# Both opening projections of a layer with the tokens stationary, and one transpose of the gated convolution input in place of two

## The chip, the cores and the metric

The kernel runs on one core of a Trainium2 chip. The metric is the device time of one execution in microseconds (us): 2051.56 us before the change, the median of three runs from 2049.41 to 2052.84.

The core's engines work side by side, each through its own queue in order: TensorE multiplies matrices into PSUM (PE in the profile; its loads of the stationary operand are PEld), VectorE (DVE) and ScalarE (ACT) do elementwise work, GpSimd (POOL) and SyncE (SP) here issue most DMAs.

## The reference, cut to what matters

A trunk of two layers on 256 tokens of width 2048. Each layer normalises its input, multiplies it by one wide weight matrix, and runs three branches on slices of the product: a sparse attention (A), a convolution (B) and a stick-breaking attention (C). Each branch is gated and projected, the three are merged by sigmoid gates, and an output projection is added to the input.

```python
h = rms_norm(x, norm_w)
proj = h @ w_in
(qa, ka, va, za, qi, ki, wi, ub, zb, qc, kc, vc, zc, gates) = jnp.split(proj, split_points(), axis=-1)

def conformer_conv(u, conv_w, conv_b, ln_w, ln_b):
    a, gt = jnp.split(u, 2, axis=-1)
    y = a * jax.nn.sigmoid(gt)
    y = depthwise_causal_conv(y, conv_w, width=31) + conv_b   # 1024 channels, along the tokens
    y = layer_norm(y, ln_w, ln_b)
    return jax.nn.silu(y)

y_b = (conformer_conv(ub, ...) * jax.nn.silu(zb)) @ w_b_out
```

What the change touches is `a * sigmoid(gt)`: 1024 channels of `a` and 1024 of `gt`, both slices of `proj`, multiplied and handed to a convolution that runs along the tokens. Everything is float32.

## The kernel before

**Precision.** Each factor of a large product is split into a high part, rounded to the matmul format, and the remainder, the low part. A product is the sum of three matmuls: high by high, low by high, high by low. ScalarE makes the high part of a weight (`high`, L219, tile `wh`), VectorE subtracts it (`low`, L223, tile `wl`).

**Units.** Weights stream through SBUF in units, mostly of two blocks of 128 rows by 512 columns (0.5 MB). SyncE loads a unit into `raw` (four buffers), `high` and `low` convert it (three buffers each), TensorE uses it. `count[0]` counts loaded units, and delays in the code are given in units.

**Two orientations.** `chunk_N` makes a product of 512 output features for 256 tokens with the activations as the stationary operand: per unit 12 matmuls, each streaming 512 columns of the weight. The result has tokens on the partitions. `chunk_T` and `chunk_first` keep the weight stationary and stream the tokens, and their result has features on the partitions. All matmuls are issued by `mult` (L233).

**The opening of a layer.** Two chunks of 512 features are computed before the normalised input exists: the first half of the gate `gt` (`ga`), then the first half of `a` (`ua`). `chunk_first` multiplies the input that is scaled by the norm's weight alone (`ux`), in 24 matmuls of 256 columns per unit, while the sum of squares is still on its way. The missing factor, one number per token, is computed meanwhile: `rsqrt_mean`, then a diagonal matrix of it (`diag_cols`, L358, tile `dg`), and one matmul with a matrix of ones (`spread`, L499) that lays it along all partitions (`rb`). In layer 0 the sum of squares is collected by VectorE (L577, L628, L629) and summed by four small matmuls (L591) in the last unit of the first chunk. In layer 1 the last quarter of the input comes from the layer before and is transposed by TensorE (L436) after the first unit. During the second chunk, `follow` makes the normalised input `hx` unit by unit (`scale_x` L484 and L487, the high copy L489, `low_x` L494), and also finishes the gate: at unit 3 VectorE multiplies `ga` by `rb` (L513) and ScalarE takes the sigmoid (L514), at unit 5 VectorE multiplies by `rb` again (L518). Behind the second chunk VectorE multiplies `ua` by that gate (L684) straight into `yT`, the convolution's input with channels on partitions. In the opening VectorE's order is the written one (in the first chunk of layer 0 also ScalarE's and TensorE's); everything else is ordered by a planner from priorities, with weight conversion at high priority.

**The second half of the convolution's input.** It comes from two `chunk_N` products with tokens on partitions, so each is turned. `turned` lets VectorE transpose blocks of 32x32 (L264, tile `zt`), stores them by four POOL DMAs to DRAM (L267, `z`), and two units later loads them back with features on partitions (L272, `zy`). A given number of units after the product (`LATER` = 9, or more or less) the data is used. `use_g` takes the sigmoid of the turned gate on ScalarE (L402), `use_a` multiplies the turned `a` by it on VectorE into `yT` (L677).

**Taps.** The convolution is 31 multiply-adds per channel block on VectorE (L420, L422). `taps` appends them, one or two to an entry, to the list `waiting`; each conversion of a unit (`low`, through `drain`) emits one entry, except during the indexer's projections. What is left is emitted at once by `flush`. Then `conv_norm` (L910 to L935) normalises in stages between units. In branch order A, C, B, both come in the second group of 512 of branch C (`j == 1`).

**Other uses of a turn that matter here.** The rotary embedding of the queries (`rope_F`) begins with two ScalarE copies of turned data (L370, L371); `use_q` scales turned data (L788); a branch's gate takes a sigmoid (L402), two VectorE products (L409, L410) and a split (L362, L363).

Of the kernel before, what the change touches and what calls it, by code (L numbers as in the profile page):

```python
# [25 lines left out]
TAPS = 31  # L26
PRE = 2
LATER = 9
EV, EV2 = (3,), (5,)
URGENT = 10 ** 6  # L30
PAD = TAPS - 1
EPS = 1e-6
# [17 lines left out]
def trunk(ctx: ExitStack, tc: tile.TileContext, x, w_in, xt, w_a, w_b, w_c, w_out,  # L50
# [29 lines left out]
    def heads(a, n):  # L80
        return a.unsqueeze(1).to_broadcast([a.shape[0], n, a.shape[-1]])
# [24 lines left out]
    def part(b, i, k, n=1, ts=slice(0, S)):  # L106
        return b[k // 4][:, k % 4:k % 4 + n, i, ts]
# [124 lines left out]
    def mult(o, lhsT, rhs, start, stop):  # L232
        newest[0] = nc.tensor.matmul(o, lhsT, rhs, start=start, stop=stop, skip_group_check=True)  # L233
        return newest[0]
# [44 lines left out]
    def by_feature(y):  # L279
        return y.rearrange("p u k i -> p k u i")  # L280

    def blocks(v):
        return v.rearrange("p k (u i) -> p k u i", i=32)

    def chunk_F(w, c0, act, nk, use, later=LATER):
        turned(chunk_N(w, [(c0, 512)], act, nk), use, later)
# [14 lines left out]
    def chunk_first(act, units):  # L301
        acc = acc_tile()
        for k0 in range(0, KD, 2):
            ks, between = units(k0)
            order = [(n, u) for n in range(3) for u in ks]
            if between:
                order = [(n, u) for u in ks for n in range(2)] + [(2, u) for u in ks]
            for m, (n, (k, w_)) in enumerate(order):
                if m == len(ks) and between:
                    between()  # L310
                j, i = ((0, 0), (0, 1), (1, 0))[n]
                for f in range(4):
                    mm = mult(acc[:, f // 2, (f % 2) * S:(f % 2) * S + S], w_[j][:, f * P:(f + 1) * P],
                              part(act, i, k)[:, 0, :], k == 0 and n == 0 and f % 2 == 0,
                              k == KD - 1 and n == 2)
            background(mm)
        return [acc[:, i, :].rearrange("p (h t) -> p h t", h=2) for i in range(2)]

    def token_products(accs, n, w_, act, k0, ku, nk, ts):
        for i, j in ((0, 0), (1, 0), (0, 1)):  # L320
# [7 lines left out]
    def chunk_N(w, segs, act, nk, ku=2):  # L328
        acc = acc_tile()
        n = sum(c for _, c in segs)  # L330
        accs = [acc[:, t, :] for t in range(NT)]
        for k0 in range(0, nk, ku):
            background(token_products(accs, n, unit(w, k0, ku, segs), act, k0, ku, nk, range(NT)))
        return accs

    def rsqrt_mean(ssum, n, buf=None):
        w_ = ssum.shape[-1]
        if buf is None:
            buf = small(8)[:, :4 * w_]
# [14 lines left out]
    def diag_cols(r):  # L354
        dg = tp.tile([P, S], F32, tag="dg", bufs=1, name=nm("dg"))
        with tc.high_priority(offset=URGENT):
            for t in range(NT):
                nc.vector.tensor_scalar(dg[:, t * P:(t + 1) * P], ident, r[:, t:t + 1], None, op0=ALU.mult)  # L358
        return dg
# [40 lines left out]
    def sigmoid_of(y):  # L400
        sg = t4().rearrange("p (u k i) -> p u k i", k=4, i=32)
        nc.scalar.activation(sg, y, AF.Sigmoid)  # L402
        return sg
# [48 lines left out]
    def ssq_total(ssq):  # L452
        s = small(2)[:, :ssq.shape[1]]
        with tc.high_priority(offset=URGENT):
            nc.vector.reduce_sum(s, ssq, axis=AX.X)
        return s
# [13 lines left out]
    for layer in range(DEPTH):  # L470
# [8 lines left out]
        with tc.manual_schedule(engines={nc.vector.engine}), ExitStack() as order:  # L479
# [24 lines left out]
            def follow(k0):  # L504
                u = k0 // 2
                if u:
                    scale_x(u - 1)
                if u > 1:
                    low_x(u - 2)
                if u in EV:  # L510
                    for i in range(2):
                        s3 = sgs[i].rearrange("p (h t) -> p h t", h=2)
                        nc.vector.tensor_mul(s3, ga[i], heads(rb, 2))  # L513
                        nc.scalar.activation(sgs[i], sgs[i], AF.Sigmoid)  # L514
                if u in EV2:
                    for i in range(2):
                        s3 = sgs[i].rearrange("p (h t) -> p h t", h=2)
                        nc.vector.tensor_mul(s3, s3, heads(rb, 2))  # L518
                return advance_units(k0)[0], None if u else lambda: spread(state["dg"])

            todo = [(k, 2, seg[0]) for k in range(0, KD, 2)] + [(k, 2, seg[1]) for k in range(0, KD, 2)]
# [66 lines left out]
            def total_square():  # L588
                ps = mm_tile()
                for t in range(NT):  # L590
                    nc.tensor.matmul(ps[:, t:t + 1], state["sum"][:, t * P:(t + 1) * P], ones[:, :1], start=True, stop=True)  # L591
                state["dg"] = diag_cols(rsqrt_mean(ps[:, :NT], D))

            def start_0(k0):
                if k0 == 0:
# [36 lines left out]
            def start_1(k0):  # L632
                if k0 == 2:
                    x_parts(x_turn(tail), xn, 12, nw, 4)
                if k0 == 14:
                    state["dg"] = diag_cols(rsqrt_mean(ssq_total(ssq), D))
                return advance_units(k0)

            if layer == 0:
# [21 lines left out]
        def taps(j, yT=yT, cv=cv, pr=pr):  # L661
            ops = []
            for c in range(j * 4, j * 4 + 4, 2):
                for q in range(TAPS):
                    for d in range(2):
                        ops.append(partial(tap, yT, cv, pr, c + d, q))
            while ops:
                n = 1 + (len(waiting) % 2 == 0)
                waiting.append([4, ops[:n]])
                ops = ops[n:]  # L670

        def use_g(y):
            sg_u.append(sigmoid_of(y))
            yield 0

        def use_a(y, yT=yT):
            nc.vector.tensor_mul(blocks(yT[:, 4:8, PAD:]), by_feature(y), by_feature(sg_u.pop()))  # L677
            taps(1)
            yield 0

        sg_u = []
        with tc.high_priority():
            for i in range(2):
                nc.vector.tensor_mul(yT[:, i * 2:i * 2 + 2, PAD:], ua[i], sgs[i].rearrange("p (h t) -> p h t", h=2))  # L684
        taps(0)
        chunk_F(w, O_UG + 4 * P, hx, KD, use_g)
        chunk_F(w, O_UA + 4 * P, hx, KD, use_a, LATER + 2)


        qi = [slot(F32R).rearrange("p a b -> p (a b)").rearrange("p (h t) -> p h t", t=P) for _ in range(2)]  # L690
# [264 lines left out]
        for b in (0, 2, 1):  # L955
            if b == 2:
                finish()
                settle()
                gc = parts(KC)
                gate(O_ZC, qcT, gc, w, hx)  # L960
            if b == 1:
                finish()
                settle()
                gb = parts(KC)
                gate(O_ZB, cv, gb, w, hx)
                mx = parts(KD)
            gx = ga if b == 0 else gc if b == 2 else gb
            for j in range(4):
                if b == 2 and j == 1:
                    finish()  # L970
                    flush()
                    start(conv_norm())
                g = chunk_N(w, [(O_G + b * D + j * 512, 512)], hx, KD)
                sg = [ev() for _ in range(NT)]
                with tc.high_priority():
                    for t in range(NT):
                        nc.scalar.activation(sg[t], g[t], AF.Sigmoid)  # L977
                if j == 0:
                    settle()
                y = chunk_N((w_a, w_b, w_c)[b][layer], [(j * 512, 512)], gx, KC)  # L980
                with tc.high_priority():
                    for t in range(NT):
                        dst = mg[j // 2][:, j % 2, t, :]
                        if b == 0:
                            nc.vector.tensor_mul(dst, y[t], sg[t])
                        else:
                            nc.vector.tensor_mul(sg[t], y[t], sg[t])  # L987
                            nc.vector.tensor_add(dst, dst, sg[t])  # L988
                if b == 1 and j < 3:
                    turned([mg[j // 2][:, j % 2, t, :] for t in range(NT)], partial(use_m, j))  # L990
                elif b == 1:
                    start(turn(j))
# [140 lines left out]
```

## Time and profile before

| | |
|---|---|
| median of three runs | 2051.56 us (2049.41 to 2052.84) |
| the profiled execution | 2050.71 us, of which the span from first to last instruction is 2048.9 |
| TensorE matmuls | 2036.2 us busy (99%), 10080 |
| TensorE weight loads | 1738.4 us (85%) |
| VectorE | 1496.9 us (73%), 2022 instructions |
| ScalarE | 1036.1 us (51%), 1217 |
| POOL | 113.1 us (6%), 189 |
| granted TensorE clock | 0.999 |
| DMA traffic | 433.00 MB, 211 GB/s on average |

Rows of a timeline give the start in us from the span's start, the duration in us (for several merged instructions, of all), the engine, the line, the operation, the tiles written and read, the shape and the count. In brackets stands how long the engine was idle before it and what ended that. A matmul's recorded duration includes its way through the pipeline; how fast matmuls follow one another is read from the starts. Layer 0 runs from 0 to about 1022 us, layer 1 from there to the end; the openings lie at 5 to 54 us and at 1022 to 1070 us.

### The profile page before, as it was taken

The numbers are of one execution on the slowest core, as the hardware profiler recorded it, in microseconds if no ns is written. First come the engines' busy times: TensorE is split into PE (matmuls) and PEld (weight loads), VectorE is DVE, ScalarE is ACT, GpSimd is POOL, SyncE is SP. The second block draws the span as 40 slices with busy tenths as digits, with TensorE's granted clock in tenths as the row PEclk, the third lists the DMA queues.
The fourth block names the chain that finished last, engine by engine and source line by source line (L and its number), as shares of the span: only waits on it lengthen the run. The fifth ranks groups of instructions, "written<-read, shape, count | busy, mean of one in ns | idle before, by whom it ended". The sixth has DMA issues, their size and how long they took to land.

```text
span 2048.9 us, 26913 instructions
## 1 busy us (share of the span) xinstructions
PE 2036.2 (99%) x10080; PEld 1738.4 (85%) x10080; DVE 1496.9 (73%) x2022; ACT 1036.1 (51%) x1217; POOL 113.1 (6%) x189
## 2 busy tenths in 40 slices
PE   9999999999999999999999999999999999999998
PEld 9899888888888888888898998888888888888887
DVE  8778998688777855655676899886887677556555
ACT  7465445466444544444454654454664445444443
POOL 0100011010000001010101001110100000011000
PEclk9999999999999999999999999999999999999999
DMA  7777577675567667876767776776755766677864
GB/s 257 228 237 216 165 240 212 196 224 165 177 197 223 195 195 225 265 234 218 243 202 230 232 199 172 247 208 195 222 165 179 207 218 192 195 237 245 252 198 147
DMA packets 245860, 433.00 MB, mean 211 GB/s; under 512 B 19552, under 2 KB 69728, under 8 KB 245600
## 3 DMA queue, kind: packets, MB, share of 16 engines
q1 hardware_dynamic: 231632, 389.32, 62.7%
q0 software_dynamic: 12432, 38.81, 6.3%
q10 hardware_dynamic: 1664, 3.15, 0.4%
q8 instruction: 79, 1.29, 0.2%
q14 instruction: 53, 0.43, 0.1%
HBM read 407.62 MB, written 23.59 MB: 210 GB/s over the span
## 4 chain that ended last, share of the span: by engine, by line
PE 47%; DVE 2%; issue 1%; DMA 0%; ACT 0%; DVEq 0%; POOLq 0%
PE acc L233 46%; DVE wl L223 1%; DVE s L422 0%; DVE sc L773 0%; PE mm L800 0%; DMA zy<-z 0%; DVE sc L726 0%; PE mm L825 0%; PE mm L894 0%; PE mm L858 0%; DVE sm L725 0%; ACT wh L219 0%; PE mm L817 0%; PE mm L880 0%; PE mm L861 0%
## 5 line engine op out<-in xcount | busy, mean ns | idle before, releaser
L233 PE MATMUL acc<-wh,s 128*128 128x512 f32 (+2 forms) x4992 | 1220.0, 387 | 1.9 <-ACT wh L219 1.9
L223 DVE TENSOR_TENSOR wl<-raw,wh 128x1024 fp32r<-128x1024 f32 (+2 forms) x729 | 876.7, 1207 | 411.8 <-ACT wh L219 409.9
L219 ACT CAST wh<-raw 128x1024 fp32r<-128x1024 f32 (+2 forms) x728 | 756.8, 1043 | 802.0 <-PE acc L233 524.2
L233 PEld LDWEIGHTS acc<-wh,s 128*128 128x128 f32 x4992 | 922.5, 188 | 187.7 <-ACT wh L219 3.0
L233 PE MATMUL acc<-wl,s 128*128 128x512 f32 (+2 forms) x2496 | 658.7, 386 | 0.6 <-DVE wl L223 0.6
L233 PEld LDWEIGHTS acc<-wl,s 128*128 128x128 f32 x2496 | 462.9, 188 | 97.6 <-DVE wl L223 4.3
L422 DVE SCALAR_TENSOR_TENSOR s<-yT,cst,s 128x256 f32<-128x256 f32 x480 | 216.2, 477 | 0.4
L233 PE MATMUL acc<-s,wh 128*128 128x256 f32 (+2 forms) x1120 | 193.4, 319 | 0.9 <-ACT wh L219 0.9
L267 POOL DMA_DIRECT2D z<-zt x148 | 86.3, 590 | 1629.0 <-DVE zt L264 1482.8
L233 PEld LDWEIGHTS acc<-s,wh 128*128 128x128 f32 x1120 | 168.4, 190 | 4.5 <-ACT wh L219 1.1
L233 PE MATMUL acc<-s,wl 128*128 128x192 f32 (+1 forms) x864 | 115.3, 276 | 0.0
L233 PEld LDWEIGHTS acc<-s,wl 128*128 128x128 f32 x864 | 112.1, 191 | 0.9
L264 DVE STREAM_TRANSPOSE zt<-acc 128x512 f32<-128x512 f32 x56 | 39.8, 710 | 14.9 <-PE acc L233 14.6
L272 POOL DMA_DIRECT2D zy<-z x37 | 26.6, 719 | 191.2 <-DMA z<-zt 121.6
L362 ACT CAST s<-zy 128x1024 fp32r<-128x1024 f32 x18 | 18.9, 1050 | 34.2 <-DMA zy<-z 17.2
L987 DVE TENSOR_TENSOR ev<-acc,ev 128x512 f32<-128x512 f32 x32 | 22.0, 687 | 17.2 <-PE acc L233 17.2
L363 DVE TENSOR_TENSOR s<-zy,s 128x1024 fp32r<-128x1024 f32 x18 | 22.0, 1223 | 16.1 <-ACT s L362 16.1
L402 ACT ACTIVATE t<-zy 128x1024 f32<-128x1024 f32 x14 | 14.9, 1061 | 29.6 <-DMA zy<-z 29.6
L409 DVE TENSOR_TENSOR zy<-zy,t 128x1024 f32<-128x1024 f32 x12 | 14.7, 1221 | 16.2 <-ACT t L402 16.2
L977 ACT ACTIVATE ev<-acc 128x512 f32<-128x512 f32 x48 | 26.3, 590 | 0.0
L387 DVE TENSOR_TENSOR ev<-ev,cst 128x384 f32<-128x384 f32 (+2 forms) x20 | 11.2, 558 | 20.4 <-ACT ev L385 20.3
L988 DVE TENSOR_TENSOR s<-s,ev 128x512 f32<-128x512 f32 x32 | 21.9, 683 | 0.0
(207 smaller groups left out, 818.1 us busy)
## 6 DMA issues: line engine op xcount, KB each, us to landing
raw<-in_w_in_dram SPq DMA_DIRECT2D x555, 512.0 KB, 3.8
raw<-in_w_out_dram SPq DMA_DIRECT2D x64, 512.0 KB, 4.7
z<-zt POOLq DMA_DIRECT2D x148, 128.0 KB, 4.4
zy<-z POOLq DMA_DIRECT2D x37, 512.0 KB, 4.9
raw<-in_w_a_dram SPq DMA_DIRECT2D x32, 512.0 KB, 3.8
raw<-in_w_c_dram SPq DMA_DIRECT2D x32, 512.0 KB, 4.4
raw<-in_w_b_dram SPq DMA_DIRECT2D x32, 512.0 KB, 5.2
raw<-in_w_in_dram SPq DMA_DIRECT2D x16, 256.0 KB, 2.9
```

The lines of the kernel that those rows point to most:

```text
L219: newest_parts[0] = nc.scalar.copy(u[1], u[0])
L223: newest_parts[1] = sub = nc.vector.tensor_sub(u[2], u[0], u[1].bitcast(F32))
L233: newest[0] = nc.tensor.matmul(o, lhsT, rhs, start=start, stop=stop, skip_group_check=True)
L264: nc.vector.transpose(tmp[:, t].rearrange("p b k i -> p k b i"), src.rearrange("p (k b c) -> p k b c", b=4, c=32))
L267: nc.gpsimd.dma_start(z[:, :, :, a, :].rearrange("t b c e -> c (t b) e"), tmp[a * 32:(a + 1) * 32].rearrange("c t b k i -> c (t b) (k i)"))
L272: nc.gpsimd.dma_start(y.rearrange("p (t a) k i -> p t (a k i)", t=n), z.rearrange("t b c a e -> (b c) t (a e)"))
L362: nc.scalar.copy(h, src)
L363: nc.vector.tensor_sub(l, src, h.bitcast(F32))
L422: nc.vector.scalar_tensor_tensor(o, yT[:, c, q:q + S], wq, o, op0=ALU.mult, op1=ALU.add)
L977: nc.scalar.activation(sg[t], g[t], AF.Sigmoid)
L987: nc.vector.tensor_mul(sg[t], y[t], sg[t])
L988: nc.vector.tensor_add(dst, dst, sg[t])
```

## The change

`chunk_first` now keeps the tokens stationary, as `chunk_N` does: per unit 12 matmuls of 512 columns in place of 24 of 256. Its two results have tokens on the partitions, where the missing factor of the norm is one number per partition (`state["r"]`). So ScalarE's sigmoid of `ga` takes it as its scale, and VectorE multiplies `ua` by the factor and the gate in one instruction. The two multiplications by `rb` fall away; `rb` itself is still made for `hx`.

The gated product `a * sigmoid(gt)` is formed with tokens on partitions for both halves, and then turned once per half: the first half right behind the opening, the second behind its two `chunk_N` products. `use_u` copies a turned half into `yT` on ScalarE and appends its taps. Before, the second half's two factors were each turned, and the first half was not turned at all. `flush` and the start of `conv_norm` move from `j == 1` to `j == 2` of branch C.

```diff
@@ chunk_first
-                for f in range(4):
-                    mm = mult(acc[:, f // 2, (f % 2) * S:(f % 2) * S + S], w_[j][:, f * P:(f + 1) * P],
-                              part(act, i, k)[:, 0, :], k == 0 and n == 0 and f % 2 == 0,
-                              k == KD - 1 and n == 2)
+                for t in range(NT):
+                    mm = mult(acc[:, t, :], part(act, i, k, 1, slice(t * P, (t + 1) * P))[:, 0, :], w_[j],
+                              k == 0 and n == 0, k == KD - 1 and n == 2)
             background(mm)
-        return [acc[:, i, :].rearrange("p (h t) -> p h t", h=2) for i in range(2)]
+        return [acc[:, t, :] for t in range(NT)]
@@ follow
-                if u in EV:
-                    for i in range(2):
-                        s3 = sgs[i].rearrange("p (h t) -> p h t", h=2)
-                        nc.vector.tensor_mul(s3, ga[i], heads(rb, 2))
-                        nc.scalar.activation(sgs[i], sgs[i], AF.Sigmoid)
-                if u in EV2:
-                    for i in range(2):
-                        s3 = sgs[i].rearrange("p (h t) -> p h t", h=2)
-                        nc.vector.tensor_mul(s3, s3, heads(rb, 2))
+                if u == 3:
+                    for t in range(NT):
+                        nc.scalar.activation(sgs[t], ga[t], AF.Sigmoid, scale=state["r"][:, t:t + 1])
@@ behind the opening
-        def use_g(y):
-            sg_u.append(sigmoid_of(y))
+        def use_u(j, y, yT=yT):
+            nc.scalar.copy(blocks(yT[:, j * 4:j * 4 + 4, PAD:]), by_feature(y))
+            taps(j)
             yield 0
-        def use_a(y, yT=yT):
-            nc.vector.tensor_mul(blocks(yT[:, 4:8, PAD:]), by_feature(y), by_feature(sg_u.pop()))
-            taps(1)
-            yield 0
         with tc.high_priority():
-            for i in range(2):
-                nc.vector.tensor_mul(yT[:, i * 2:i * 2 + 2, PAD:], ua[i], sgs[i].rearrange("p (h t) -> p h t", h=2))
-        taps(0)
-        chunk_F(w, O_UG + 4 * P, hx, KD, use_g)
-        chunk_F(w, O_UA + 4 * P, hx, KD, use_a, LATER + 2)
+            for t in range(NT):
+                nc.vector.scalar_tensor_tensor(sgs[t], ua[t], state["r"][:, t:t + 1], sgs[t], op0=ALU.mult, op1=ALU.mult)
+        turned(sgs, partial(use_u, 0))
+        g = chunk_N(w, [(O_UG + 4 * P, 512)], hx, KD)
+        sgs = [ev() for _ in range(NT)]
+        with tc.high_priority():
+            for t in range(NT):
+                nc.scalar.activation(sgs[t], g[t], AF.Sigmoid)
+        a = chunk_N(w, [(O_UA + 4 * P, 512)], hx, KD)
+        with tc.high_priority():
+            for t in range(NT):
+                nc.vector.tensor_mul(sgs[t], a[t], sgs[t])
+        turned(sgs, partial(use_u, 1), LATER + 2)
@@ branch C
-                if b == 2 and j == 1:
+                if b == 2 and j == 2:
                     finish()
                     flush()
                     start(conv_norm())
```

More of the change, by code (lines that the diff above doesn't have):

```diff
@@ L28 @@
 LATER = 9
-EV, EV2 = (3,), (5,)
 URGENT = 10 ** 6
@@ L591, in total_square @@
                     nc.tensor.matmul(ps[:, t:t + 1], state["sum"][:, t * P:(t + 1) * P], ones[:, :1], start=True, stop=True)
-                state["dg"] = diag_cols(rsqrt_mean(ps[:, :NT], D))
+                state["r"] = rsqrt_mean(ps[:, :NT], D)
+                state["dg"] = diag_cols(state["r"])
             def start_0(k0):
@@ L635, in start_1 @@
                 if k0 == 14:
-                    state["dg"] = diag_cols(rsqrt_mean(ssq_total(ssq), D))
+                    state["r"] = rsqrt_mean(ssq_total(ssq), D)
+                    state["dg"] = diag_cols(state["r"])
                 return advance_units(k0)
@@ L670, in taps @@
                 ops = ops[n:]
-        def use_g(y):
-            sg_u.append(sigmoid_of(y))
+        def use_u(j, y, yT=yT):
+            nc.scalar.copy(blocks(yT[:, j * 4:j * 4 + 4, PAD:]), by_feature(y))
+            taps(j)
             yield 0
-        def use_a(y, yT=yT):
-            nc.vector.tensor_mul(blocks(yT[:, 4:8, PAD:]), by_feature(y), by_feature(sg_u.pop()))
-            taps(1)
-            yield 0
-        sg_u = []
-        with tc.high_priority():
-            for i in range(2):
-                nc.vector.tensor_mul(yT[:, i * 2:i * 2 + 2, PAD:], ua[i], sgs[i].rearrange("p (h t) -> p h t", h=2))
-        taps(0)
-        chunk_F(w, O_UG + 4 * P, hx, KD, use_g)
-        chunk_F(w, O_UA + 4 * P, hx, KD, use_a, LATER + 2)
+        with tc.high_priority():
+            for t in range(NT):
[11 more added lines that the diff above has]
+        turned(sgs, partial(use_u, 1), LATER + 2)
         qi = [slot(F32R).rearrange("p a b -> p (a b)").rearrange("p (h t) -> p h t", t=P) for _ in range(2)]
```

## The prediction

> **What bounds the kernel now.** I read the page's totals first, then TensorE's list of waits, then the timelines of TensorE and VectorE through both openings, and last the round trips through the DRAM scratch.
>
> ```profile
> span 2048.9 us, 26913 instructions
> ...
> PE 2036.2 (99%) x10080; PEld 1738.4 (85%) x10080; DVE 1496.9 (73%) x2022; ACT 1036.1 (51%) x1217; POOL 113.1 (6%) x189
> ```
>
> Matmuls fill 99% of the span. TensorE's waits (engine and line, what released it, us in total, times, longest):
>
> ```profile
> PE acc L233 <- ACT wh L219: 2.8, 3, 1.1
> ...
> PE acc L233 <- DVE wl L223: 0.6, 2, 0.3
> PE mm L436 <- DVE t L1021: 0.3, 1, 0.3
> ```
>
> These come to 3.7 us in 2049. So TensorE sets the time nearly everywhere, and the question is what the opening costs TensorE before and after. Its timeline (start, us, engine, line, operation, count, and the idle time before it):
>
> ```profile
> 9.13 2.18 PE L233 MATMUL acc<-s,wh 128*128 128x256 f32 x16 [0.93 <-ACT wh L219]
> ...
> 26.51 1.12 PE L233 MATMUL acc<-s,wh 128*128 128x256 f32 x8
> 27.66 0.61 PE L591 MATMUL mm<-cst,t 128*128 128x1 f32 x4
> ...
> 33.43 2.08 PE L233 MATMUL acc<-s,wh 128*128 128x256 f32 x16
> ...
> 53.59 2.00 PE L233 MATMUL acc<-wh,s 128*128 128x512 f32 x8
> ...
> 56.34 1.98 PE L233 MATMUL acc<-wh,s 128*128 128x512 f32 x8
> ...
> 75.38 1.98 PE L233 MATMUL acc<-wh,s 128*128 128x512 f32 x8
> ```
>
> A unit is two blocks of 128 rows of the weight by 512 columns. In the opening it is 24 matmuls of 256 columns: from 33.43 to 53.59 lie 7 units, 2.880 us each, 120 ns a matmul. From 56.34 to 75.38 lie 7 units of a tokens-stationary projection, 12 matmuls of 512 columns each: 2.720 us, 227 ns a matmul. Twice 120 is 240: at the same number of columns each matmul carries some 13 ns that do not depend on its length. The changed opening issues just the second form.
>
> **Term 1, the openings on TensorE.** The change takes 12 matmuls out of each of 32 units (four chunks of eight), 384 in all, and 0.160 us out of each unit: 5.1 us, if TensorE is the limit in every one. So I go through the four chunks.
>
> Layer 0, first chunk. After the first third of its last unit TensorE needs the sum of squares, which VectorE makes:
>
> ```profile
> 18.91 1.22 DVE L223 TENSOR_TENSOR wl<-raw,wh 128x1024 fp32r<-128x1024 f32 x1
> ...
> 25.71 0.68 DVE L577 TENSOR_TENSOR t<-t,t 128x512 f32<-128x512 f32 x1
> ...
> 27.19 0.41 DVE L629 TENSOR_TENSOR t<-t 128x256 f32<-128x256 f32 x1
> ...
> 29.63 0.48 DVE L358 TENSOR_SCALAR dg<-cst,sm 128x128 f32<-128x128 f32 x2
> ```
>
> VectorE shows no wait from 18.91 to the end of L629 at 27.60, and L591 starts at 27.66, while the matmuls before it end at about 27.47 (8 x 0.120 from 26.51). TensorE waits there already. Made faster by 0.16 us in each of six units from 9.13 on, it comes about 1 us sooner and waits 1.2 us instead of 0.2. So of this chunk I count only the 16 matmuls behind the sum: 16 x 0.120 - 8 x 0.227 = 0.10 us. Lower end 0; upper end 1.3 (all eight units), if VectorE's order lets the sum come sooner.
>
> Layer 0, second chunk: 8 x 0.160 = 1.28 us. The spread of the scales, a matmul from dg behind its first eight matmuls, is reached 0.15 us sooner than now, near 30.9; dg is there at 30.11. VectorE's own pace here:
>
> ```profile
> 38.77 1.29 DVE L513 TENSOR_TENSOR ev<-acc,rb 128x512 f32<-128x512 f32 x2
> ...
> 41.10 0.88 DVE L487 SCALAR_TENSOR_TENSOR s<-s,x0n,rb 128x256 f32<-128x256 f32 x2
> ...
> 43.63 0.88 DVE L487 SCALAR_TENSOR_TENSOR s<-s,x0n,rb 128x256 f32<-128x256 f32 x2
> ...
> 45.03 1.29 DVE L518 TENSOR_TENSOR ev<-ev,rb 128x512 f32<-128x512 f32 x2
> ...
> 55.89 0.69 DVE L684 TENSOR_TENSOR yT<-acc,ev 128x512 f32<-128x512 f32 x1
> ```
>
> A unit of VectorE's fixed work is 2.53 us (41.10 to 43.63), under 2.72, and the change removes L513 and L518, 2.58 us per layer. VectorE holds the pace. The two sigmoids stay on ScalarE; they now read PSUM with the scale as an operand.
>
> Layer 1:
>
> ```profile
> 1024.68 1.28 DVE L1021 TENSOR_TENSOR t<-acc,t 128x512 f32<-128x512 f32 x2
> ...
> 1026.02 0.98 PE L436 MATMUL mm<-cst,t 128*128 128x128 f32 x7 [0.27 <-DVE t L1021]
> 1026.76 2.16 PE L233 MATMUL acc<-s,wh 128*128 128x256 f32 x16
> ...
> 1070.45 2.00 PE L233 MATMUL acc<-wh,s 128*128 128x512 f32 x8
> ```
>
> After its first unit TensorE turns the last quarter of x and waits for L1021, so that unit's 0.16 goes into the wait. The other 15 units run from 1026.76 to 1070.45, with only the spread's two matmuls between them: 15 x 0.160 = 2.40 us.
>
> Term 1: 0.10 + 1.28 + 2.40 = 3.8 us gained; ends 3.7 and 5.1.
>
> [...]
>
> **Term 2, the end of the convolution.** The first half of its input now makes a round trip, so its taps start later, and the normalisation starts one group of 512 later (j == 2):
>
> ```profile
> 611.04 0.48 DVE L422 SCALAR_TENSOR_TENSOR s<-yT,cst,s 128x256 f32<-128x256 f32 x1
> ...
> 653.36 2.01 DVE L910 TENSOR_REDUCE t<-s 128x256 f32<-128x1024 f32 x1
> 655.29 1.21 DVE L363 TENSOR_TENSOR s<-zy,s 128x1024 fp32r<-128x1024 f32 x1
> ```
>
> and on TensorE:
>
> ```profile
> 655.53 2.22 PE L233 MATMUL acc<-wh,s 128*128 128x512 f32 x8
> ...
> 658.74 2.01 PE L233 MATMUL acc<-wh,s 128*128 128x512 f32 x8
> ```
>
> The last tap of layer 0 runs at 611. One entry of the list goes per unit, and the list now starts about nine units later, so it ends near 611 + 9 x 2.72 = 636, before the group j == 1, which begins two units behind 658.74, at 664: nothing is flushed in a burst. The reduction L910, pulled forward, stands ahead of L363, for which the unit at 655.53 waits: 3.21 us in place of 2.72. Moved by a group, L910 meets no such chain. I count 0.5 us; ends 0, if another operation takes its place, and 0.5. Taps between 611 and 636 lie beside the gate of branch C; today's taps lie beside the gate of branch A, and the list of waits has none from them.
>
> **Term 3, the round trip.** There are still two turns per layer, each with four stores, one load and the same work on POOL's queue; but the first now comes right behind the opening. On it hangs a new ScalarE copy of 128x1024 into yT, and the weight casts queue behind that copy. Such trips now:
>
> ```profile
> 75.58 0.72 DVE L264 STREAM_TRANSPOSE zt<-acc 128x512 f32<-128x512 f32 x1 [0.92 <-PE acc L233]
> 77.32 0.71 DVE L264 STREAM_TRANSPOSE zt<-acc 128x512 f32<-128x512 f32 x1
> ...
> 85.82 0.72 POOL L272 DMA_DIRECT2D zy<-z  x1 [5.04 <-DMA z<-zt]
> ...
> 91.95 1.06 ACT L402 ACTIVATE t<-zy 128x1024 f32<-128x1024 f32 x1
> ...
> 256.83 1.99 PE L233 MATMUL acc<-wh,s 128*128 128x512 f32 x8
> ...
> 272.06 1.05 ACT L370 COPY t<-zy 64x1024 f32<-64x1024 f32 x1 [4.72 <-DMA zy<-z]
> ...
> 274.23 2.11 PE L233 MATMUL acc<-wh,s 128*128 128x512 f32 x8 [0.75 <-ACT wh L219]
> ...
> 296.04 1.06 ACT L788 ACTIVATE s<-zy 128x1024 f32<-128x1024 f32 x1 [3.92 <-DMA zy<-z]
> ```
>
> At 91.95 ScalarE reached a use with the same lag of 9 units, without waiting, 16.6 us after TensorE began the next chunk (75.38). The new turn starts from two VectorE multiplies, today's L684, the last of which ends 3.0 us after TensorE left the chunk (56.58 against 53.59). A turn's two transposes of 0.7 us, with a subtract between them, bring that to 4.4 to 5.6; in the rows above it is 2.65 (78.03 against 75.38). So the data lands 1.8 to 3.0 us later than there, and ScalarE may wait some 2 us. The rows price a wait: 3.92 us appears with no idle TensorE on the list, 4.72 us with 0.75. Up to about 4 us ScalarE's lead covers it, and beyond that a microsecond of wait costs about one. I take 0, by the nearest row, 91.95. The other end: the use at 272.06, with a lag of 8, was reached at 267.34, 10.5 us after 256.83; one unit more makes 13.2, and against a landing 17 to 18 us in, the wait is 4 to 5 us, a loss of up to 1.2 per layer, 2.4 in all.
>
> The second turn replaces one ScalarE sigmoid and one VectorE product of 1024 columns by two of each of 512, and adds a copy; ScalarE, 51% busy, gains about 2 us per layer beside the matmuls. VectorE's lighter opening is worth nothing further, since TensorE does not wait for it there.
>
> **Sum.** 3.8 + 0.5 - 0 = 4.3 us. The profiled execution took 2050.71 us, its span 2048.9, which gives 2046.4; it lay 0.85 under the median 2051.56 of the three runs, which gives 2047.3. I write 2046.9, between them.
>
> **Rivals.** (1) The copy blocks the casts. If the load lands later than I think, TensorE stops in both layers. The gain is used up when ScalarE waits about 6.1 us in each layer (2 x 2.1 beyond 4), and the kernel is slower by 0.2% at about 8.2 (2 x 4.2), at 2055.8. For it: 4.72 us occurs now. Against: the lag is a unit longer here, and the nearest row waits for nothing. Chance 0.20.
>
> (2) The waits behind the opening go. Of the 3.4 us in the list's first two rows 0.93 lie at the start; the other 2.5 lie where index selection, rotary and taps share VectorE and L370 blocks the casts. The taps reach that stage about nine entries further back, so the order there can shift. If all of it goes: 2044.4. For: these are TensorE's only larger waits. Against: one entry goes per unit there as before, and L370's load is not moved. Chance 0.18.
>
> (3) The change does not do what it says: TensorE's time goes by columns, 240 ns for 512 in this place as twice 120 now, and term 1 is 0. Then only term 2 is left: 2050.7. Against: the rows at 56.34 and after have the same form at 227. Chance 0.10. [...]
>
> **How the numbers follow.** Forecast 0.52, from 2045.6 (term 1's upper end) to 2049.8 (2.4 and 0.5 lost). 0.2% is 4.1 us, about what a measurement of this kernel can tell from no change; the limit at 2047.5 cuts the forecast into 0.37 faster and 0.15 no change. Rival 1 gives 0.01, 0.07 and 0.12; rival 2 gives 0.17, 0.01 and 0; rival 3 gives 0, 0.10 and 0. Sum: 0.55, 0.33, 0.12. The range, 2043.5 to 2052.0, reaches from rival 2 with a part of term 1's upper end to rival 1 at its break-even; outside lies the worse half of rival 1.
>
> **What would show it.** TensorE with 9696 matmuls; units of the opening at 2.72 us; about 1.2 us of waiting before L591's successor; 2.4 us less between the turn of x and the end of layer 1's opening; no long unit near 655; ScalarE's wait for zy behind the opening under 4 us. I am wrong if the opening's units stay near 2.88, if TensorE idles for a cast that stands behind the new copy, or if the index stage shows new waits.

## The result: 0.2% faster, nearly all of it in the opening

The changed kernel takes 2050.09 us (median of 13 runs, 2046.86 to 2053.22); the kernel before, measured beside it, 2053.93 us (13 runs, 2049.41 to 2057.57). The ratio is 0.9982, 95% interval [0.9975, 0.9989]: 3.7 us less, between 2.3 and 5.1.

The page of the changed kernel, its totals:

```profile
span 2048.2 us, 26153 instructions
...
PE 2032.1 (99%) x9696; PEld 1718.2 (84%) x9696; DVE 1490.5 (73%) x2016; ACT 1039.4 (51%) x1223; POOL 113.6 (6%) x189
```

384 matmuls and six VectorE instructions are gone, and ScalarE has six more, as the parts of the change add up. Now the list of TensorE's waits (engine and line, what released it, us in total, times, longest). The lines have moved: L218 is the cast to high, L232 the matmul, L222 the low part, L583 the sum of squares, L434 the turn of x.

```profile
PE acc L232 <- ACT wh L218: 4.5, 5, 1.9
...
PE mm L583 <- DVE t L622: 1.0, 1, 1.0
PE mm L434 <- DVE t L1019: 0.8, 2, 0.6
PE acc L232 <- DVE wl L222: 0.8, 2, 0.4
```

The waits grew: 4.5 us behind ScalarE's casts in place of 2.8, 0.8 at the turn of x in place of 0.3, and a new 1.0 at the sum of squares. TensorE's timeline through both openings:

```profile
28.08 0.61 PE L583 MATMUL mm<-cst,t 128*128 128x1 f32 x4 [0.97 <-DVE t L622]
...
33.67 1.98 PE L232 MATMUL acc<-wh,s 128*128 128x512 f32 x8
...
52.71 1.98 PE L232 MATMUL acc<-wh,s 128*128 128x512 f32 x8
...
1027.85 2.09 PE L232 MATMUL acc<-wh,s 128*128 128x512 f32 x8
...
1069.24 1.98 PE L232 MATMUL acc<-wh,s 128*128 128x512 f32 x8
```

Seven units lie between 33.67 and 52.71, 2.720 us each. From the sum of squares to the start of the next projection layer 0 took 25.93 us (27.66 to 53.59) and takes 24.63 (28.08 to 52.71): 1.30 less. From the first matmul behind the turn of x, layer 1 took 43.69 (1026.76 to 1070.45) and takes 41.39: 2.30 less. Together 3.6 us, close to the 3.7 us of the ratio; the interval is too wide (2.3 to 5.1) for the closeness itself to say much.

Yet these two profiled executions differ by 0.6 us only (2050.71 and 2050.09). The place where the changed one lost is far from the change, at the second half of branch B's gate, where ScalarE's sigmoid waits for turned data. ScalarE and TensorE there, in the changed kernel:

```profile
824.15 1.06 ACT L400 ACTIVATE t<-zy 128x1024 f32<-128x1024 f32 x1 [7.87 <-DMA zy<-z]
826.19 2.11 PE L232 MATMUL acc<-wh,s 128*128 128x512 f32 x8 [1.94 <-ACT wh L218]
...
1839.91 1.06 ACT L400 ACTIVATE t<-zy 128x1024 f32<-128x1024 f32 x1 [7.17 <-DMA zy<-z]
1841.95 2.12 PE L232 MATMUL acc<-wh,s 128*128 128x512 f32 x8 [1.24 <-ACT wh L218]
```

and ScalarE at the same place in the profile before:

```profile
822.56 1.06 ACT L402 ACTIVATE t<-zy 128x1024 f32<-128x1024 f32 x1 [4.75 <-DMA zy<-z]
```

There the data came after 4.75 us (5.83 in layer 1), and no idle TensorE followed in either layer. So 3.2 us of idle TensorE (1.94 + 1.24) stand in one profile and not in the other. Whether the change made them was the first thing to settle.

### The profile page after: what moved, and what is told of

The parts are those of the page before. It is cut to its first block, busy times and chain, and to the rows that moved or that the text cites. A ratio compares the mean times of both kernels' runs of the same rounds, so it can differ in the third digit from the quotient of the medians.

```text
span 2048.2 us, 26153 instructions
## 1 busy us (share of the span) xinstructions
PE 2032.1 (99%) x9696; PEld 1718.2 (84%) x9696; DVE 1490.5 (73%) x2016; ACT 1039.4 (51%) x1223; POOL 113.6 (6%) x189
## 4 chain that ended last, share of the span: by engine, by line
PE 47%; DVE 2%; DMA 1%; issue 1%; ACT 0%; POOL 0%; DVEq 0%; POOLq 0%; ACTq 0%
PE acc L232 45%; DVE wl L222 1%; DMA zy<-z 1%; DMA z<-zt 0%; PE mm L765 0%; PE mm L798 0%; DVE s L420 0%; ACT wh L218 0%; PE mm L823 0%; PE mm L892 0%; PE mm L856 0%; DVE sc L724 0%; PE mm L815 0%; DVE sm L723 0%; PE mm L878 0%
## 5 line engine op out<-in xcount | busy, mean ns | idle before, releaser
L232 PE MATMUL acc<-wh,s 128*128 128x512 f32 (+2 forms) x5248 | 1285.1, 387 | 4.5 <-ACT wh L218 4.5
L222 DVE TENSOR_TENSOR wl<-raw,wh 128x1024 fp32r<-128x1024 f32 (+2 forms) x729 | 876.1, 1206 | 408.6 <-ACT wh L218 407.6
L218 ACT CAST wh<-raw 128x1024 fp32r<-128x1024 f32 (+2 forms) x728 | 756.5, 1043 | 790.5 <-PE acc L232 529.0
L232 PEld LDWEIGHTS acc<-wh,s 128*128 128x128 f32 x5248 | 970.6, 188 | 201.5 <-ACT wh L218 6.6
L232 PE MATMUL acc<-wl,s 128*128 128x512 f32 (+2 forms) x2624 | 692.3, 386 | 0.8 <-DVE wl L222 0.8
L232 PEld LDWEIGHTS acc<-wl,s 128*128 128x128 f32 x2624 | 486.9, 188 | 102.5 <-DVE wl L222 3.9
L232 PE MATMUL acc<-s,wh 128*128 128x384 f32 (+1 forms) x608 | 125.6, 347 | 0.0
L232 PEld LDWEIGHTS acc<-s,wh 128*128 128x128 f32 x608 | 104.3, 189 | 3.2
L232 PEld LDWEIGHTS acc<-s,wl 128*128 128x128 f32 x608 | 79.1, 191 | 0.9
L232 PE MATMUL acc<-s,wl 128*128 128x192 f32 (+1 forms) x608 | 79.4, 273 | 0.0
L263 DVE STREAM_TRANSPOSE zt<-acc 128x512 f32<-128x512 f32 x48 | 34.0, 709 | 8.2 <-PE acc L232 8.1
```

What stands on the lines that cost most here:

```text
L218: newest_parts[0] = nc.scalar.copy(u[1], u[0])
L222: newest_parts[1] = sub = nc.vector.tensor_sub(u[2], u[0], u[1].bitcast(F32))
L263: nc.vector.transpose(tmp[:, t].rearrange("p b k i -> p k b i"), src.rearrange("p (k b c) -> p k b c", b=4, c=32))
```

## The experiments

Three theories. T (what it says of the gate is theory A in the expectations below): the gain is the shorter units, the rest of the change is worth nothing, and the gate of branch B varies from one execution to the next in both kernels. B: the later normalisation made the gate's wait longer, so that a better version keeps the change and loses the wait. R: the time goes by columns, and the gain comes from elsewhere.

### Both kernels once more

No edit. First the kernel before:

> The kernel before, unchanged, profiled in a second execution. Theory A (the prediction's terms hold, and what the two profiles lack, 0.7 us instead of 4.3, is a wait that differs between executions of either kernel): ratio 1.000, and the wait of ScalarE for its turned gate in branch B near 822 and 1841 us differs from the 4.75 and 5.7 us of the first profile by a microsecond or more, with idle TensorE when it is longer. Theory B (the later normalisation or the new order makes that wait longer): the waits are again 4.8 and 5.7 us within 0.3.

and the changed kernel:

> The kernel after, unchanged, profiled in a second execution. Theory A: 3.5 to 4.5 us faster than before (ratio 0.998), and the waits for the turned gate of branch B, 7.87 and 7.17 us in the first profile, come out differently by a microsecond or more. Theory B: they are again 7 to 8 us, and TensorE loses 1.2 to 2 us at each.

The kernel before took 2052.65 us, ratio to its other runs 0.9993 [0.9985, 1.0002]; the changed kernel 2049.78 us, 0.998 [0.9971, 0.9989]. The second profile of the kernel before, ScalarE and then TensorE at the gate:

```profile
823.80 1.06 ACT L402 ACTIVATE t<-zy 128x1024 f32<-128x1024 f32 x1 [6.63 <-DMA zy<-z]
...
825.84 2.11 PE L233 MATMUL acc<-wh,s 128*128 128x512 f32 x8 [0.70 <-ACT wh L219]
```

In layer 1 of this profile the wait is 7.16 us and TensorE idles 1.23. The second profile of the changed kernel has waits of 7.59 and 5.93 us there, with 1.66 us of idle TensorE and none. So the stop is in the kernel before too: it is a load that lands earlier in one execution and later in another. Whether the change adds a part is not settled. At the two gates together TensorE idles 0, 1.9 and 3.3 us in the three profiles that were taken with the old opening, and 1.3 to 4.4 us (3.0 on average) in the six with the new one that leave the gate where it is; so few profiles cannot exclude a microsecond.

The second profile of the kernel before also has no long unit at the place where the prediction had seen one (655.53 to 658.74, 3.21 us):

```profile
655.41 1.98 PE L233 MATMUL acc<-wh,s 128*128 128x512 f32 x8
...
658.13 1.98 PE L233 MATMUL acc<-wh,s 128*128 128x512 f32 x8
```

2.72 us. What term 2 counted was an event of one execution.

### Half the columns per matmul

The changed kernel with each matmul of the opening split into two of 256 columns; tokens stay stationary, all else is as in the changed kernel.

```diff
-                    mm = mult(acc[:, t, :], part(...)[:, 0, :], w_[j], k == 0 and n == 0, k == KD - 1 and n == 2)
+                    for f in range(2):
+                        mm = mult(acc[:, t, f * S:(f + 1) * S], part(...)[:, 0, :],
+                                  w_[j][:, f * S:(f + 1) * S], k == 0 and n == 0 and f == 0, k == KD - 1 and n == 2)
```

> The kernel after, but each matmul of the opening split into two of 256 columns with the same stationary operand, so 24 per unit as before: term 1 alone undone. Prediction (13 ns per matmul whatever its length): units of the opening at 2.88 us again, 3.6 to 3.8 us slower than the kernel after, so within 1 us of the kernel before (ratio 0.9995 to 1.000). Rival 3 (time goes by columns): units at 2.72 us and the time of the kernel after (ratio 0.998).

2052.85 us, ratio 0.9995 [0.9986, 1.0004]: 3.1 us above the changed kernel's 2049.78 on the same chip, and level with the kernel before. TensorE's timeline of this kernel:

```profile
33.67 2.08 PE L232 MATMUL acc<-wh,s 128*128 128x256 f32 x16
...
50.95 2.08 PE L232 MATMUL acc<-wh,s 128*128 128x256 f32 x16
```

Six units in 17.28 us: 2.88 us each, the old pace with the new orientation. So the number and length of the matmuls, not the orientation, made the gain, and theory R falls. Each matmul comes with its own load of the stationary operand (9696 loads in the changed kernel, 10080 again here), so these runs do not tell whether the 13 ns belong to the matmul or to the load. All that the change does beside it (fewer VectorE multiplications, one turn in place of two factors, the later normalisation) leaves a ratio that cannot be told from 1.

### The normalisation, in both kernels

The changed kernel with the start of the normalisation back at the second group, and the kernel before with it at the third:

```diff
 # the changed kernel
-                if b == 2 and j == 2:
+                if b == 2 and j == 1:
 # the kernel before
-                if b == 2 and j == 1:
+                if b == 2 and j == 2:
```

> The kernel after with the normalisation back at j == 1: term 2 alone undone. Prediction: the long unit near 655 us comes back, 0.5 us slower than the kernel after (ratio to before 0.9984). Theory B (the later normalisation lengthens the wait at the gate of branch B): the waits there fall to about 5 us, and it is 2 to 3.5 us faster than the kernel after (ratio 0.9965 to 0.997).

> The kernel before with only the start of the normalisation moved to j == 2: term 2 alone done. Prediction as written: 0.5 us faster than before (ratio 0.9998). What the second profile of the kernel before suggests instead (the long unit near 655 us belongs to one execution): no difference, ratio 1.000, with an interval that holds 1.

The changed kernel with the early normalisation took 2050.48 us, ratio 0.9988 [0.9976, 1.0]; the kernel before with the late one 2053.0 us, ratio 1.0001 [0.9992, 1.0009]. The first has no long unit near 655, and ScalarE still waits 7.84 and 7.96 us at branch B's gate, where theory B asked for about 5, with a stop of TensorE in both layers. So theory B falls. The prediction's term 2 has nothing left to rest on, as the long unit is absent with the early normalisation too; its 0.5 us is smaller than both intervals, so a gain of that size is not excluded, only not seen. The first of these runs also shows the new copy waiting longer than in the profile above; ScalarE, then TensorE beside it:

```profile
73.84 1.05 ACT L667 COPY yT<-zy 128x1024 f32<-128x1024 f32 x1 [5.06 <-DMA zy<-z]
...
73.87 1.98 PE L232 MATMUL acc<-wh,s 128*128 128x512 f32 x8
75.69 1.07 PE L232 MATMUL acc<-wl,s 128*128 128x512 f32 x4
76.59 1.98 PE L232 MATMUL acc<-wh,s 128*128 128x512 f32 x8
```

5.06 us of wait, and TensorE's units still follow at 2.72. The prediction would have put one microsecond there.

### The new copy earlier, a first attempt

To price the copy's wait, its due time was set two units earlier:

```diff
-        turned(sgs, partial(use_u, 0))
+        turned(sgs, partial(use_u, 0), LATER - 2)
```

> The kernel after with the first half's copy into yT two units sooner in the order (a lag of 7 units for 9): rival 1 made to happen. ScalarE reaches the copy 5.4 us sooner, so its wait rises from 1.2 and 1.5 us to 6.6 to 7.5. Price as in the prediction (each microsecond beyond 4 costs TensorE one): TensorE idles 2.5 to 3.5 us behind each opening, 5 to 7 us slower than the kernel after. Price as the first profile after shows it at the gate of branch B (7.87 us of wait cost 1.9 to 2.1, so beyond about 5.8): 0.8 to 1.7 us at each, 2 to 3 us slower.

2049.47 us, ratio 0.9986 [0.9974, 0.9998]. The planner did not do what was meant; ScalarE in layer 0:

```profile
71.90 1.05 ACT L667 COPY yT<-zy 128x1024 f32<-128x1024 f32 x1 [2.83 <-DMA zy<-z]
```

The casts still ran ahead of the copy, so its wait is in the range of the other runs and says nothing on the price of a longer one. A due time is a wish here; only a dependence fixes the order.

### The new copy earlier, by order

The same, and the next weight cast may only be issued behind the copy, which puts two weight casts that stood ahead of it behind it:

```diff
+    ahead = []
-        with tc.high_priority():
+        with tc.high_priority(), tc.issue_after(ahead.pop().ins) if ahead else nullcontext():
             ...                                  # the high cast of a unit
-            nc.scalar.copy(blocks(yT[:, j * 4:j * 4 + 4, PAD:]), by_feature(y))
+            cp_ = nc.scalar.copy(blocks(yT[:, j * 4:j * 4 + 4, PAD:]), by_feature(y))
+            if j == 0:
+                ahead.append(cp_)
-        turned(sgs, partial(use_u, 0))
+        turned(sgs, partial(use_u, 0), LATER - 2)
```

> The changed kernel with the new copy two weight casts further ahead in ScalarE's order, in both openings, so that ScalarE comes to it about 5.4 us sooner and waits 6.6 to 7.5 us there in place of 1.2 to 1.5. By the prediction's price (what is beyond 4 us is TensorE's) each opening loses 2.5 to 3.5 us: 5 to 7 us more than the changed kernel, ratio to the kernel before about 1.001. By the rows of the gate of branch B (what is beyond about 5.8 us is TensorE's) each loses 0.8 to 1.7 us: 2 to 3 us more, ratio 0.999 to 0.9995. If two weight tiles ahead of TensorE are more cushion than that, nothing is lost and the ratio stays at 0.998.

2055.78 us (11 runs, 2051.83 to 2060.38), ratio 1.0013 [1.0003, 1.0023]: slower than the kernel before. This is the prediction's first rival, made to happen. ScalarE at both copies and TensorE behind them:

```profile
71.43 1.04 ACT L668 COPY yT<-zy 128x1024 f32<-128x1024 f32 x1 [8.07 <-DMA zy<-z]
...
73.47 2.76 PE L233 MATMUL acc<-wh,s 128*128 128x512 f32 x8 [2.18 <-ACT wh L219]
76.03 1.91 PE L233 MATMUL acc<-wl,s 128*128 128x512 f32 x4
77.74 2.21 PE L233 MATMUL acc<-wh,s 128*128 128x512 f32 x8
...
1091.78 1.05 ACT L668 COPY yT<-zy 128x1024 f32<-128x1024 f32 x1 [7.30 <-DMA zy<-z]
...
1093.82 2.14 PE L233 MATMUL acc<-wh,s 128*128 128x512 f32 x8 [1.37 <-ACT wh L219]
```

A wait of 8.07 us idles TensorE 2.18 us, one of 7.30 us 1.37: in both, what is beyond 5.9 us. That is the price of branch B's gate, not the prediction's 4 us. But the sum is nearer to the prediction's, because of what comes behind the first stop. The four low matmuls at 76.03 start 2.56 us after the eight before them, where 1.81 is usual. The windows of this kernel from the end of the stop on (columns: PE, PEld, DVE, ACT and POOL busy with counts, then the granted clock, DMA share, GB/s):

```profile
73.40:76.00 2.60, 2.53 (x8) 2.03 (x9) 2.55 (x3) 1.91 (x3) 0.00 (x0) 0.76 0.11 15
76.00:79.00 3.00, 3.00 (x10) 2.35 (x9) 1.91 (x2) 2.07 (x3) 0.00 (x0) 0.64 0.91 271
```

After the idle 2.18 us the granted clock fell to 0.76 and 0.64 in these windows: 0.24 x 2.6 + 0.36 x 3.0 = 1.7 us of clock. So the stop of 2.18 us cost some 3.9, while that of 1.37 us left the clock at 1.00. The two copies cost 2.18 + 1.37 + 1.7 = 5.3 us; the expectation from the gate's price was 2 to 3, from the prediction's 5 to 7, and the measured distance of the ratios, 1.0013 - 0.9982, is 6.4 us. In this profile the turn of x also stopped TensorE, 2.0 us in two waits in place of 0.8, and the eight matmuls behind it are slow as well (3.58 us in place of 2.09 at 1027.85 in the changed kernel), since the granted clock is 0.54 from 1030.20 to 1033.80 us, another 1.7 us lost (0.46 x 3.6; the last row has the columns of the windows above):

```profile
1028.93 0.33 PE L435 MATMUL mm<-cst,t 128*128 128x128 f32 x1 [1.73 <-DVE t L1022]
1029.53 0.98 PE L435 MATMUL mm<-cst,t 128*128 128x128 f32 x7 [0.27 <-DVE t L1022]
1030.27 3.58 PE L233 MATMUL acc<-wh,s 128*128 128x512 f32 x8
...
1030.20:1033.80 3.60, 3.60 (x12) 2.83 (x11) 2.49 (x3) 2.42 (x4) 0.00 (x0) 0.54 0.93 296
```

So part of the distance to the changed kernel is not the copies'.

### Branch B's gate one unit later

The changed kernel with the second half of branch B's gate used at `LATER` in place of `LATER - 1`. Since `settle()` in branch B's first group takes all that is pending at once, it is left out for that branch.

```diff
-            chunk_F(w, c0 + k * P, hx, KD, partial(use, k), LATER - 1)
+            chunk_F(w, c0 + k * P, hx, KD, partial(use, k), LATER - (c0 != O_ZB or k == 0))
...
-                if j == 0:
+                if j == 0 and b != 1:
                     settle()
```

> The kernel after with the use of branch B's second turned gate half one unit later in the order, between the first units of the projection behind it, so that one more weight cast stands ahead of ScalarE's wait. If the idle TensorE there (2.1 and 1.4 us, then 1.8 and 0 in the two profiles) comes from the wait ahead of the casts, it goes: 2 to 3 us faster than the kernel after, ratio to before 0.9965 to 0.997. If the late data itself holds up the projection, the idle time moves to a later unit and the time stays at 0.998.

2047.23 us, ratio 0.9972 [0.9962, 0.9982]. ScalarE at the gate:

```profile
820.43 1.06 ACT L400 ACTIVATE t<-zy 128x1024 f32<-128x1024 f32 x1 [2.21 <-DMA zy<-z]
...
1835.68 1.06 ACT L400 ACTIVATE t<-zy 128x1024 f32<-128x1024 f32 x1 [2.37 <-DMA zy<-z]
```

One more cast stands ahead of the sigmoid, the wait falls from over 7 us to 2.3, and TensorE no longer stops in either layer. The cast accounts for a unit's 2.7 us of that at most; the load also landed sooner: TensorE is 0.8 us ahead of the changed kernel here (the unit that starts at 815.92 there starts at 815.15), the sigmoid 3.7 us (824.15 there, 820.43 here), and why was not tried. The interval lies clear of the kernel before; against the changed kernel (0.9982 [0.9975, 0.9989]) it is 0.10% lower with intervals that overlap, and the two kernels built on it below stand at the same place. The same once more for the queries' rotary embedding (`rope_F`, first step at `LATER`), on top of it:

```diff
-            chunk_F(w, O_QA + h * P, hx, KD, partial(rope_F, qaT[:, h:h + 4, :]), LATER - 1)
+            chunk_F(w, O_QA + h * P, hx, KD, partial(rope_F, qaT[:, h:h + 4, :]), LATER)
```

> The kernel of the run before this in the list, and the first step of the queries' rotary embedding also one unit later in the order. Its waits cost TensorE 0.6 and 0.5, and 0.6 and 1.7 us in the two profiles after. If they go too, it is 1 to 2 us faster still, ratio to before 0.996; if VectorE's load in the index stage is what holds TensorE there, it is the same within 0.5 us.

2046.99 us, 0.9971 [0.996, 0.9983]: no further gain. The stops behind ScalarE at 272 and 1290 us went, and those behind VectorE's low part grew from 0.4 to 1.0 us, at 258 and at 1274.

### The two waits that the shorter units left

On top of the later gate: the sum-of-squares matmuls after two thirds of layer 0's last unit of the first chunk, and the turn of x in layer 1 one unit later.

```diff
-                if m == len(ks) and between:
+                if m == len(ks) * (1 + (k0 == KD - 2)) and between:
...
-                if k0 == 2:
+                if k0 == 4:
                     x_parts(x_turn(tail), xn, 12, nw, 4)
```

> The kernel with the later gate, and beside it the two waits that the shorter opening units left: the sum-of-squares matmuls of layer 0 a third of a unit later, the turn of x in layer 1 one unit later. If these waits are VectorE's lateness at one place, they go (1.0 us at 27 to 28 us, 0.8 to 1.9 us at 1022 to 1027 us, no other takes their place) and the kernel is about 2 us quicker than the one with the later gate alone: ratio to the kernel before 0.9962 to 0.9965. If VectorE's chain is itself what layer 0's start waits for, the wait only moves to the spread of the scale behind it or to the next weight cast, and the gain is 0.5 us or less: ratio 0.997.

2046.14 us (6 runs), ratio 0.9968 [0.9956, 0.998]. Both waits are gone from the list, and one has come up in the third unit behind the sum of squares; ScalarE, VectorE and TensorE there:

```profile
35.28 0.36 ACT L498 COPY rb<-mm 128x256 f32<-128x256 f32 x1
...
35.68 0.88 DVE L485 SCALAR_TENSOR_TENSOR s<-s,x0n,rb 128x256 f32<-128x256 f32 x2 [4.45 <-ACT rb L498]
...
38.54 1.19 PE L232 MATMUL acc<-wl,s 128*128 128x512 f32 x4 [1.53 <-DVE wl L222]
```

In layer 0 the wait moved to the scale behind the sum, as the second expectation had it. VectorE stood idle 4.45 us for `rb`, the spread scale, and made its next low part late. ScalarE copied `rb` at 35.28, behind a third weight cast; in the changed kernel it did so at 33.97, behind two. In layer 1 nothing took the place of the wait at the turn of x. The upper end of the interval, 0.998, lies just under the changed kernel's 0.9982, but that kernel's own interval begins at 0.9975, so the two overlap; with the later gate alone the overlap is almost whole, and the step of 1.1 us between those two is not shown. It has the lowest median of all kernels run.

## Why the prediction was right, point by point

It named 2046.9 us and 4.3 us of gain; measured were 3.7 us. The absolute time lies 3.2 us higher largely because the runs beside the changed kernel put the kernel before at 2053.93, not at 2051.56. At 2050.09 it is just above the forecast's own band (2045.6 to 2049.8) and close to rival 3's 2050.7, so it is the units and the split matmuls, not the absolute time, that speak for the mechanism. The chances gave 0.55 to a gain of more than 4.1 us; the measured 3.7 is just short of that, in the part that got 0.33.

**Term 1, right.** 1.28 + 0.10 was said for layer 0, 1.30 came; 2.40 for layer 1, 2.30 came. Splitting the matmuls gave the gain back (3.1 us). That only a part of the first chunk counts was right too: 1.2 us of wait was forecast before the matmul behind the sum of squares, and the row at 28.08 has 0.97.

**Term 2, the step that failed.** "I count 0.5 us" for the normalisation's move: the long unit near 655 was in one execution, not in the second of the same kernel, and moving the normalisation alone made no difference that could be measured in either kernel. A single long unit was read as a property of the order.

**Term 3, the right size by a wrong price.** The copy waited 1.21 and 1.46 us in the first profile, here in layer 0:

```profile
70.59 1.05 ACT L667 COPY yT<-zy 128x1024 f32<-128x1024 f32 x1 [1.21 <-DMA zy<-z]
```

and up to 5.06 in another, where "under 4" was said; it cost nothing in any. "Up to about 4 us ScalarE's lead covers it" was taken from the queries' place, where a stop of 0.75 follows a wait of 4.72. At the new copy and at branch B's gate the lead is 5.9 us. The difference is how far ahead of TensorE ScalarE's last cast stood when the wait began. The queries' place in the profile before:

```profile
266.28 1.05 ACT L219 CAST wh<-raw 128x1024 fp32r<-128x1024 f32 x1 [2.71 <-DMA raw<-in_w_in_dram]
...
270.60 1.98 PE L233 MATMUL acc<-wh,s 128*128 128x512 f32 x8
...
273.13 1.05 ACT L219 CAST wh<-raw 128x1024 fp32r<-128x1024 f32 x1
```

and the gate in the changed kernel:

```profile
815.22 1.05 ACT L218 CAST wh<-raw 128x1024 fp32r<-128x1024 f32 x1 [1.67 <-PE acc L232]
...
821.37 1.98 PE L232 MATMUL acc<-wh,s 128*128 128x512 f32 x8
```

The last cast before the wait began 4.3 us ahead of its unit (266.28, 270.60) at the queries and 6.2 us ahead (815.22, 821.37) at the gate; with the copy placed by order it was 6.1 (62.30, 68.41). At the queries that cast had itself waited for the raw weights to land. In both places one operation of about a microsecond, and then the next cast, follows the wait (273.13 lies between the two copies), so the rest of the way is nearly the same. The row for the price came from a place where ScalarE was less far ahead. "Beyond that a microsecond of wait costs about one" holds for TensorE's idle time alone; the 1.7 us at a granted clock of 0.76 and 0.64 that came behind the stop of 2.18 us the prediction did not have.

**The rivals.** The first, the copy blocks the casts: its mechanism is real, and when it was forced the kernel turned slower. Its prediction for 8.07 and 7.30 us of wait would be 7.4 us (4.1 + 3.3); the profile shows 5.3. In the changed kernel as it stands the waits (1.2 to 4.7 us in its two profiles) never reach the 5.9 us. The second, the index stage's waits go: they stayed, near 255, 273, 1272 and 1290 us (together 1.6 and 2.7 us in the two profiles of the changed kernel, 2.4 in both of the kernel before). The third, time by columns: shown wrong.

One reading at the start was short: "These come to 3.7 us" leaves out a line of the same list, 1.1 us at the very beginning (L604, ahead of the first 20 matmuls on the tile `idle`), so all waits come to 4.8. Every kernel here has that wait, and nothing in the sum rests on it.

## What to carry to other kernels

Before a stop of a microsecond is put down to an edit, look whether it is there in a second execution of the kernel without it: here 3.2 us came and went with the landing of a load, in both kernels, and so did the 0.5 us of a term of the forecast. A wait on an engine that feeds the bound engine is priced at its own place, as the wait less the work that is converted ahead (here what is beyond 4.0 us at the queries and 5.9 at the gate), and a consumer that stands just short of that limit is worth trying one unit later even when the profile at hand shows no loss there. Where a matmul carries a fixed cost (some 13 ns here, an estimate from 120 ns at 256 columns and 227 at 512), count instructions in the stage that TensorE bounds, and then see which producers it now outruns: each of them takes back a part.

## What the runs showed of the hardware beyond that

**The granted clock fell behind some stops of TensorE and not behind others.** Behind the stop of 2.18 us it was 0.76 and 0.64 in the two windows above (73.40 to 79.00 us), 1.7 us of lost clock. Behind the stop of 1.37 us it was 1.00 (1093.80 to 1096.00), and also behind that of 1.94 us in the changed kernel (826.10 to 829.00). The matmuls were slow behind stops of 2.62 us (the early normalisation, at 275.01) and 2.59 us (the copy's first attempt, at 826.73) too: the four low matmuls start 3.39 and 3.21 us after the eight before them, where it is 1.95 behind the stop of 1.94 us. Two other stops are of nearly the same length. The changed kernel with the early normalisation at the gate in layer 1:

```profile
1844.65 3.18 PE L232 MATMUL acc<-wh,s 128*128 128x512 f32 x8 [2.03 <-ACT wh L218]
1847.63 1.64 PE L232 MATMUL acc<-wl,s 128*128 128x512 f32 x4
```

and the kernel before with the late normalisation, in layer 0:

```profile
827.61 2.11 PE L233 MATMUL acc<-wh,s 128*128 128x512 f32 x8 [2.08 <-ACT wh L219]
829.56 1.08 PE L233 MATMUL acc<-wl,s 128*128 128x512 f32 x4
```

After 2.03 us the low matmuls start 2.98 us later, after 2.08 us 1.95. So the length of the stop alone does not decide. At the turn of x above, waits of 1.73 and 0.27 us, with one matmul of 0.33 us between them, were followed by a granted clock of 0.54. What decides beside the length was not shown.

**The same load lands at very different times.** At branch B's gate, at the same place in ScalarE's order, the wait was 4.75 to 7.96 us in the executions whose gate was not moved. Waits of up to 5.9 us left TensorE all but unstopped; those of 6.6 us and more stopped it, in 12 of 14 cases for what was beyond 5.93, and twice (7.32 and 7.58 us) for 0.7 and 0.9 us more than that. What delays the load was not tried and stays open.
